# A streaming add-and-GELU kernel: wider chunks, longer store rows, and a first store that is issued later

## The chip, the cores and the metric

One core of one Trainium2 chip. The metric is the device time of one launch in microseconds. All runs quoted here were fast, with a granted clock of 1.0. The span is the part of a launch that is profiled, from the program's first instruction to its last. Differences in this case are of the order of 0.5%, so every comparison has four to six timed runs of the changed kernel and six to eleven of the kernel before, in alternation and, on each occasion, on one chip. A ratio is the mean time of one kernel's fast runs over that of the other's of the same rounds, so it is not quite the ratio of the medians quoted beside it; it comes with its 95% interval.

## The reference

```python
# x, y: (1024, 4096) float32
z = x + y
out = 0.5 * z * (1 + np.tanh(np.sqrt(2 / np.pi) * (z + 0.044715 * z ** 3)))
```

33.55 MB are read and 16.78 MB written. The kernel uses 0.5 (1 + tanh(u)) = sigmoid(2u), so an element takes an add, a square, a scalar-tensor operation, a sigmoid and a multiplication.

## The kernel before

Each of the 128 partitions holds eight rows, 32,768 columns, in one SBUF tile `z`. All transfers are issued by one sequencer (SP) on one queue. The adds run on GpSimd (the first on VectorE), squares and sigmoids on ScalarE, the other two operations on VectorE; `w` is in PSUM.

```python
    YS = 8192
    CH = 1024
    PS = 4
    loads = [2048, 6144, 8192, 8192, 8192]
    stores = [8192, 8192, 8192, 4096, 4096]
    # ... pools: z for all columns, two y buffers of YS columns, PS PSUM buffers of CH columns
    def store(i):
        a, b = sr[i]
        nc.sync.dma_start(out=ov[:, a:b], in_=zt[:, a:b])
    # ...
    sp = []
    for i in range(len(loads)):
        sp += [(load_x, i), (load_y, i)]
    sp += [(store, i) for i in range(len(stores))]
    # ...
    for i in range(-3, C + 1):
        if 0 <= i < C:
            dve.append((stt, i))
            acts.append((sig, i))
        if 0 <= i - 1 < C:
            dve.append((mul, i - 1))
        # ...
        if 0 <= i + 2 < C:
            acts.append((sq, i + 2))
    # ...
        store: lambda i: [(mul, c) for c in over(cr, *sr[i])],
```

## Time and profile before

| | before |
|---|---|
| device time, median | 122.09 us |
| span of the profiled run | 119.9 us |
| share of the 16 DMA engines' span filled by the one queue | 98.4% |
| first store issued / last load complete | 60.5 us / 80.7 us |
| last compute instruction ends | 103.9 us |

Three more lines of the page and the timeline of the kernel before matter later. The first counts packets, the second is a second DMA queue (its packets, MB, share of the engines' span), the third the issue of the stores (start, length, instruction, number).

```profile
DMA packets 2162, 50.35 MB, mean 420 GB/s; under 512 B 240, under 2 KB 240, under 8 KB 240
...
q14 instruction: 2, 0.02, 0.0%
```

```profile
60.52 43.78 SPq L131 DMA_DIRECT2D out_dram<-z  x5
```

Of 2162 packets, 2160 carry data or completions. The other two are 8 KB each on the queue that brings instructions.

### The profile page before, as it was taken

The numbers are of one execution on the slowest core, as the hardware profiler recorded it, in microseconds if no ns is written. First come the engines' busy times: TensorE is split into PE (matmuls) and PEld (weight loads), VectorE is DVE, ScalarE is ACT, GpSimd is POOL, SyncE is SP. The second block draws the span as 40 slices with busy tenths as digits, with TensorE's granted clock in tenths as the row PEclk, the third lists the DMA queues.
The fourth block names the chain that finished last, engine by engine and source line by source line (L and its number), as shares of the span: only waits on it lengthen the run. The fifth ranks groups of instructions, "written<-read, shape, count | busy, mean of one in ns | idle before, by whom it ended". The sixth has DMA issues, their size and how long they took to land.

```text
span 119.9 us, 247 instructions
## 1 busy us (share of the span) xinstructions
DVE 75.5 (63%) x66; ACT 63.8 (53%) x66; POOL 73.0 (61%) x35
## 2 busy tenths in 40 slices
DVE  0044700049999109999996999996899999600000
ACT  4006300078876038788867887884888887200000
POOL 0046000699990199999969999959999991000000
DMA  6999999989898999999898989999998989998995
GB/s 191 424 478 410 476 426 394 514 361 514 361 503 372 481 394 448 426 426 448 383 492 372 503 350 514 361 383 481 388 481 372 492 383 481 394 470 366 437 426 224
DMA packets 2162, 50.35 MB, mean 420 GB/s; under 512 B 240, under 2 KB 240, under 8 KB 240
## 3 DMA queue, kind: packets, MB, share of 16 engines
q1 hardware_dynamic: 2160, 50.33, 98.4%
q14 instruction: 2, 0.02, 0.0%
HBM read 33.55 MB, written 16.78 MB: 420 GB/s over the span
## 4 chain that ended last, share of the span: by engine, by line
DMA 49%; POOL 17%; DVE 16%; SPq 1%; ACT 1%; issue 0%; POOLq 0%
DMA y<-in_y_dram 49%; POOL z L137 17%; DVE z L157 8%; DVE w L148 8%; ACT w L142 1%; SPq L120 1%; SPq L127 1%; POOLq L137 0%
## 5 line engine op out<-in xcount | busy, mean ns | idle before, releaser
L137 POOL TENSOR_TENSOR z<-z,y 128x1024 f32<-128x1024 f32 x31 | 72.8, 2388 | 26.1 <-DMA y<-in_y_dram 26.1
L142 ACT ACTIVATE w<-z 128x1024 f32<-128x1024 f32 x32 | 32.9, 1028 | 37.3 <-POOL z L137 31.3
L148 DVE SCALAR_TENSOR_TENSOR w<-w,z 128x1024 f32<-128x1024 f32 x32 | 39.4, 1233 | 21.0 <-ACT w L142 21.0
L157 DVE TENSOR_TENSOR z<-w,z 128x1024 f32<-128x1024 f32 x32 | 38.8, 1215 | 0.0
L153 ACT ACTIVATE w<-w 128x1024 f32<-128x1024 f32 x32 | 31.4, 981 | 0.4 <-DVE w L148 0.4
L137 DVE TENSOR_TENSOR z<-z,y 128x1024 f32<-128x1024 f32 x1 | 1.2, 1226 | 6.1 <-DMA y<-in_y_dram 6.1
L196 ACT ACT_TABLE_LOAD x1 | 1.3, 1283 | 1.3 <-PEq L228 1.3
L195 DVE MEMSET one<- 128x1 f32 x1 | 0.1, 59 | 1.3 <-PEq L228 1.3
L228 POOL MEMSET const-float32-0.0<- 128x1 f32 x1 | 0.1, 98 | 0.2 <-issue 0.2
L196 ACT ACTIVATE one<-one 128x1 f32<-128x1 f32 x1 | 0.2, 203 | 0.0
L228 POOL MEMSET const-bfloat16-1.0<- 128x1 bf16 x1 | 0.1, 101 | 0.0
L228 POOL MEMSET const-uint8-127<- 128x1 uint8 x1 | 0.1, 101 | 0.0
L228 POOL MEMSET const-float32-1.0<- 128x1 f32 x1 | 0.1, 98 | 0.0
## 6 DMA issues: line engine op xcount, KB each, us to landing
z<-in_x_dram SPq DMA_DIRECT2D x3, 4096.0 KB, 34.2
y<-in_y_dram SPq DMA_DIRECT2D x3, 4096.0 KB, 24.8
out_dram<-z SPq DMA_DIRECT2D x3, 4096.0 KB, 30.2
out_dram<-z SPq DMA_DIRECT2D x2, 2048.0 KB, 17.3
z<-in_x_dram SPq DMA_DIRECT2D x1, 3072.0 KB, 13.4
y<-in_y_dram SPq DMA_DIRECT2D x1, 3072.0 KB, 20.4
z<-in_x_dram SPq DMA_DIRECT2D x1, 1024.0 KB, 4.9
y<-in_y_dram SPq DMA_DIRECT2D x1, 1024.0 KB, 7.0
```

What stands on the lines that cost most here:

```text
L120: nc.sync.dma_start(out=zt[:, a:b], in_=xv[:, a:b])
L127: nc.sync.dma_start(out=yt[s][:, o : o + b - a], in_=yv[:, a:b])
L137: eng.tensor_add(out=zt[:, a:b], in0=zt[:, a:b], in1=yt[s][:, o : o + b - a])
L142: nc.scalar.activation(out=wt[c], in_=zt[:, a:b], func=act.Square, scale=root)
L148: nc.vector.scalar_tensor_tensor(out=wt[c], in0=wt[c], scalar=c1, in1=zt[:, a:b], op0=alu.add, op1=alu.mult)
L153: nc.scalar.activation(out=wt[c], in_=wt[c], func=act.Sigmoid)
L157: nc.vector.tensor_mul(out=zt[:, a:b], in0=wt[c], in1=zt[:, a:b])
L195: nc.vector.memset(one, 0.0)
L196: nc.scalar.activation(out=one, in_=one, func=act.Sigmoid)
L228: nc = _bacc.Bacc("TRN2", target_bir_lowering=False, num_devices=1)
```

## The change

Its intent: fewer, longer instructions and rows, and stores that join the queue only when the loads are nearly through. Cut to its core:

```diff
-    CH = 1024
-    PS = 4
+    CH = 2048
+    PS = 2
     loads = [2048, 6144, 8192, 8192, 8192]
-    stores = [8192, 8192, 8192, 4096, 4096]
+    FIRST = 8
+    stores = [16384, 8192, 4096, 4096]
 ...
-        nc.sync.dma_start(out=ov[:, a:b], in_=zt[:, a:b])
+        ins = nc.sync.dma_start(out=ov[:, a:b], in_=zt[:, a:b])
+        if i == 0:
+            tc.add_manual_dep(ins.ins, muls[FIRST].name, ...)
 ...
-    for i in range(-3, C + 1):
-        ...
+    acts = [(sq, 0), (sq, 1)]
+    for c in range(0, C, 2):
+        dve += [(stt, c), (stt, c + 1), (mul, c), (mul, c + 1)]
+        acts += [(sig, c), (sig, c + 1)]
+        if c + 2 < C:
+            acts += [(sq, c + 2), (sq, c + 3)]
 ...
-        store: lambda i: [(mul, c) for c in over(cr, *sr[i])],
+        store: lambda i: [(mul, c) for c in over(cr, *sr[i])] + [(mul, FIRST)],
```

More of the change, by code (lines that the diff above doesn't have):

```diff
@@ L115 @@
     zt = pool_sb.tile([P, TOT], fp32, tag="z", name="z")
-    yt, wt = {}, {}
+    yt, wt, muls = {}, {}, {}
     def load_x(i):
@@ L130, in store @@
         a, b = sr[i]
-        nc.sync.dma_start(out=ov[:, a:b], in_=zt[:, a:b])
+        ins = nc.sync.dma_start(out=ov[:, a:b], in_=zt[:, a:b])
+        if i == 0:
+            tc.add_manual_dep(
+                ins.ins,
+                muls[FIRST].name,
+                mybir.DependencyInfo(mybir.DependencyClass.Sync, mybir.DependencyReason.DATA),
+                reason="the stores join the queue when the last load is nearly done",
+            )
     def add(c):
@@ L156, in mul @@
         a, b = cr[c]
-        nc.vector.tensor_mul(out=zt[:, a:b], in0=wt[c], in1=zt[:, a:b])
+        muls[c] = nc.vector.tensor_mul(out=zt[:, a:b], in0=wt[c], in1=zt[:, a:b]).ins
     sp = []
@@ L164 @@
     pool = [(add, c) for c in range(C) if c in by_pool]
-    dve, acts = [], []
-    for i in range(-3, C + 1):
-        if 0 <= i < C:
-            dve.append((stt, i))
-            acts.append((sig, i))
-        if 0 <= i - 1 < C:
-            dve.append((mul, i - 1))
-        if 0 <= i + 3 < C and i + 3 not in by_pool:
-            dve.append((add, i + 3))
-        if 0 <= i + 2 < C:
-            acts.append((sq, i + 2))
+    dve = [(add, c) for c in range(C) if c not in by_pool]
+    acts = [(sq, 0), (sq, 1)]
[4 more added lines that the diff above has]
+            acts += [(sq, c + 2), (sq, c + 3)]
     needs = {
```

## The prediction

> **What bounds the kernel now.** I read the page first, the slices (part 2) before the groups of instructions, because no compute engine there is busy over two thirds of the span.
>
> ```profile
> DVE 75.5 (63%) x66; ACT 63.8 (53%) x66; POOL 73.0 (61%) x35
> ...
> DVE  0044700049999109999996999996899999600000
> ACT  4006300078876038788867887884888887200000
> POOL 0046000699990199999969999959999991000000
> DMA  6999999989898999999898989999998989998995
> ...
> q1 hardware_dynamic: 2160, 50.33, 98.4%
> ...
> HBM read 33.55 MB, written 16.78 MB: 420 GB/s over the span
> ```
>
> Every compute engine has holes; the DMA row has none. From the second slice to the last but one it reads 8 or 9, and the one queue's packets fill 98.4% of 16 engines' span. The transfers are the bound, and the bytes (x and y in, the result out) are fixed.
>
> The chain of waits has to be read with this in mind: it follows the last instructions, and its last piece, the final multiplications, ends at 101.64 + 2.30 = 103.9 us of a span of 119.9. The last 16 us are stores alone. The waits of the DMA queue's own sequencer and the chain tell whether the queue ever runs short of work:
>
> ```profile
> SPq L131 <- DVE z L157: 41.8, 4, 19.4
> SPq L127 <- POOL z L137: 32.6, 2, 18.6
> ```
>
> ```profile
> 2.87 38.57 DMA y<-in_y_dram
> ...
> 41.56 18.51 POOL z L137 x8
> ...
> 60.09 20.58 DMA y<-in_y_dram
> ...
> 101.64 2.30 DVE z L157 x2
> ```
>
> The sequencer waits long, but for transfers that are wanted later. The fourth y load is issued at 60.09 us, when GpSimd has freed its buffer, and in the timeline the first store at 60.52. Both stand behind an x load issued at 36.4, so the engines work on: by stretches, the five from 7 to 104 us move 427, 432, 430, 424 and 433 GB/s. Loads end at about 80.7 us, and stores take the rest. Their last issue is at 104.0, some 16 us before the end, so compute is not what they wait for.
>
> Where do 119.9 us go on a DMA engine? The trace's packet records give the median of one row: 309 ns for 8 KB, 611 for 16, 912 for 24, 1213 for 32. That is a line: (1213 - 309) / 3 = 301.3 ns per 8 KB, and about 8 ns a packet. One engine (an equal sixteenth of the packets) has 16 x 0.309 + 16 x 0.912 + 72 x 1.213 + 16 x 0.611 us, and 15 completion packets of 9 ns: 116.8 us. Beside this there is 1.5 us before the first packet, 0.6 us per engine by which the first load packets are longer than the median, and **0.46 us per engine at 77 to 80 us, where the last two load packets of many engines are longer (up to 1.87 us) as the engines turn from loads to stores**. The completions of the last load come over 0.76 us instead of 0.54, those of the later stores over 0.9. So some 0.5 to 1 us is all that scheduling of the stores could ever recover.
>
> **What the Trainium skill says.** "DMA: Bandwidth & Descriptors", section "Where 436 GB/s comes from", has 435.2 GB/s as the ceiling of the 16 ports; the trace agrees (32 KB in 1.213 us on 16 engines is 432 GB/s), so a full engine has no faster rate to find. The same page, "Queues, rings and completion order", says that an engine consumes descriptors in ring order; the trace agrees, stores of 4 MB being 30.2 us from issue to landing in the median, where 4 MB alone take about 10. "GPSIMD Engine Reference", section 3.1, has 4497 ns on GpSimd and 2293 ns on the vector engine for an add of 2048 fp32 columns. Those are my durations for the new shapes; the trace has 2388 and 1226 ns for 1024, so the doubled ones fit. "SBUF — State Buffer", section "Who interferes with whom", says that a vector instruction with two SBUF inputs contends with a GpSimd one that reads SBUF: at 7.5 us the trace has both adding, and GpSimd's first took 3.39 us instead of about 2.3.
>
> **The change, part by part.**
>
> *Chunks of 2048.* Each engine has half the instructions at about twice the length. Starts of consecutive vector instructions lie 1.14 to 1.15 us apart in the timeline, and the second 1024 columns cost 2293 - 1226 = 1067 ns more by the two figures above; so one of 2048 takes 1.145 + 1.067 = about 2.2 us, against 2.29 for two. ScalarE goes from 0.96 to an estimated 1.9 (at most twice), GpSimd from 2.31 to about 4.5. With 64 vector instructions turned into 32, this saves 32 x 0.08 = 2.6 us of vector time, and GpSimd 15 x 0.1 = 1.5; none of it is on the path, since transfers set the end. The first add becomes 2048 on the vector engine with no GpSimd add beside it: also hidden.
>
> *Two PSUM buffers, pairs.* The order list has squares for c and c+1, two scalar-tensor operations, two sigmoids, two multiplications. The square of c+2 now waits for the multiplication of c. With 2.2 us of the other multiplication to cover a square of 1.9, the vector engine should stay nearly full, 8.8 us per pair against 9.0 of GpSimd adds. This coarsens the pipeline, and chunk 15 finishes later: from the last y at 80.7, four adds of 4.5 end at 98.9; square 100.8, scalar-tensor 103.1, two multiplications 107.5. That is 3.5 us later than before, but the stores behind it need it only at about 115.
>
> *The late store.* It waits for chunk 8's multiplication, the third of its group of four vector instructions. The x and y for it land at 61.0 (GpSimd's start in the trace). Adds of chunks 8 and 9 end at 65.6 and 70.1; the square of 9 at 72; its scalar-tensor at 74.3; the multiplication of 8 follows at 76.5. So the store is issued at about 76.6 rather than 60.5. From first issue to first packet the trace took 1.5 us: data at about 78. The engines finish their loads at 80.0 to 80.7, so they should find the store there, **with about 2 us to spare**. The next stores: chunk 11 is done at about 88 (the first store occupies the queue until 100), chunk 13 at 98.5 (needed at 110), chunk 15 at 107.5 (needed at 115). No hole.
>
> *64 KB rows.* 128 / 16 = 8 rows per engine replace 16 of 32 KB: by the line, 2419 ns instead of 2 x 1213, saving 8 x 0.008 = 0.06 us, and one completion packet less. Together **0.07 us**.
>
> Sum: -0.07 us, and between -0.5 and +0.5 for how the turn from loads to stores goes. I take -0.1: 122.0.
>
> **The rivals.** (1) *The turn gets cheaper.* If the longer packets at 77 to 80 us and the uneven completions come from the store descriptors lying behind the loads for 17 us, the late issue removes them: 0.5 us, 121.5 at best perhaps 121.2. For it: the excess lies exactly at the turn. Against: descriptors also lie queued from 36 us on without any excess, and the store is to be there before the turn in both kernels. (2) *The queue runs dry.* If the pair order costs more than I counted, or if a store with such long rows takes longer to start, each us beyond 80 us is a us lost on all engines: 2 us late would give 124. For it: a margin of only 2 us, hanging on six dependent instructions. Against: all six have measured durations. (3) *64 KB rows are slower or get split.* A split in two gives the old time; anything odd at this size would show in 8 rows per engine, 10% over their 19.4 us being 2 us. The line from 8 to 32 KB gives no sign of it. (4) *Compute becomes the bound at the end.* It would need chunk 15 to come 7 us later than worked out; unlikely.
>
> **Range and chances.** The spread of three runs is 0.02 us, other boots perhaps 0.3%. Rivals 1 and 2 set the ends: 121.3 to 122.8. Faster by 2% means 119.6 us or less, below what 116.8 us of packets and the fixed ends allow: 0.01. Slower by 2% needs a hole of 2.4 us by rival 2 or 3: 0.04.
>
> **What would show it.** DMA row without a hole, queue share still above 98%; first store issued at 76 to 78 us; completions of the last load at the same time as before, near 80.7; packets of 64 KB at about 2.42 us; last vector instruction at 107 to 108; GpSimd adds near 4.5 us. A gap between the last load packet and the first store packet proves rival 2; the excess at 77 to 80 us gone proves rival 1.

## The result

The changed kernel takes **121.61 us** (median of 6, 121.37 to 121.98) against 122.09 (6 runs): ratio 0.9965, interval 0.9942 to 0.9988. That is 0.4 us faster: well under 2%, and inside the range. The page of the changed kernel:

```profile
DVE 73.7 (62%) x34; ACT 61.0 (51%) x34; POOL 67.5 (56%) x19
...
DMA  6999999989898999989898989998899889999996
...
DMA packets 2016, 50.33 MB, mean 420 GB/s; under 512 B 224, under 2 KB 224, under 8 KB 224
...
q1 hardware_dynamic: 2016, 50.33, 98.6%
...
L145 POOL TENSOR_TENSOR z<-z,y 128x2048 f32<-128x2048 f32 x15 | 67.3, 4519 | 31.1 <-DMA y<-in_y_dram 31.1
L156 DVE SCALAR_TENSOR_TENSOR w<-w,z 128x2048 f32<-128x2048 f32 x16 | 36.7, 2296 | 26.4 <-ACT w L150 26.1
```

The DMA row has no hole in either kernel, and the queue's share hardly moved. All 2016 packets are the data queue's: **there is no q14 line here any more**. From its timeline, the issue of the stores and the last multiplications:

```profile
76.44 31.41 SPq L132 DMA_DIRECT2D out_dram<-z  x4
...
103.01 4.48 DVE L165 TENSOR_TENSOR z<-w,z 128x2048 f32<-128x2048 f32 x2
```

The first store goes out 16 us later than before, and compute ends at 107.5 us instead of 103.9. Neither made the kernel slower.

The profiled executions do not show where the 0.4 us went: that of the kernel before, from another occasion than the six runs, happened to be a quick one (121.73 us, below their median), that of the changed kernel a slow one (121.92, above its own). A gain as small as the scatter of one kernel's runs can't be read off one pair of profiles. It needs runs that take the parts apart.

### The profile page after: what moved, and what is told of

Read it like the earlier page. It is cut to its first block, busy times and chain, and to the rows that moved or that the text cites. A ratio compares the mean times of both kernels' runs of the same rounds, so it can differ in the third digit from the quotient of the medians.

```text
span 119.8 us, 174 instructions
## 1 busy us (share of the span) xinstructions
DVE 73.7 (62%) x34; ACT 61.0 (51%) x34; POOL 67.5 (56%) x19
## 2 busy tenths in 40 slices
DMA packets 2016, 50.33 MB, mean 420 GB/s; under 512 B 224, under 2 KB 224, under 8 KB 224
## 3 DMA queue, kind: packets, MB, share of 16 engines
q1 hardware_dynamic: 2016, 50.33, 98.6%
## 4 chain that ended last, share of the span: by engine, by line
DMA 50%; POOL 26%; POOLq 4%; DVE 4%; DVEq 2%; ACT 2%; SPq 1%; issue 0%
DMA y<-in_y_dram 50%; POOL z L145 26%; POOLq L215 4%; DVE w L156 2%; DVEq L215 2%; DVE z L165 2%; ACT w L150 2%; SPq L121 1%; SPq L128 1%; POOLq L145 0%
## 5 line engine op out<-in xcount | busy, mean ns | idle before, releaser
L145 POOL TENSOR_TENSOR z<-z,y 128x2048 f32<-128x2048 f32 x15 | 67.3, 4519 | 31.1 <-DMA y<-in_y_dram 31.1
L156 DVE SCALAR_TENSOR_TENSOR w<-w,z 128x2048 f32<-128x2048 f32 x16 | 36.7, 2296 | 26.4 <-ACT w L150 26.1
L150 ACT ACTIVATE w<-z 128x2048 f32<-128x2048 f32 x16 | 30.1, 1882 | 38.3 <-POOL z L145 29.3
L165 DVE TENSOR_TENSOR z<-w,z 128x2048 f32<-128x2048 f32 x16 | 35.8, 2281 | 0.0
L161 ACT ACTIVATE w<-w 128x2048 f32<-128x2048 f32 x16 | 29.7, 1855 | 4.4 <-DVE w L156 4.4
L145 DVE TENSOR_TENSOR z<-z,y 128x2048 f32<-128x2048 f32 x1 | 2.3, 2293 | 6.1 <-DMA y<-in_y_dram 6.1
```

Of the source, the lines that this page charges most:

```text
L145: eng.tensor_add(out=zt[:, a:b], in0=zt[:, a:b], in1=yt[s][:, o : o + b - a])
L150: nc.scalar.activation(out=wt[c], in_=zt[:, a:b], func=act.Square, scale=root)
L156: nc.vector.scalar_tensor_tensor(out=wt[c], in0=wt[c], scalar=c1, in1=zt[:, a:b], op0=alu.add, op1=alu.mult)
L161: nc.scalar.activation(out=wt[c], in_=wt[c], func=act.Sigmoid)
L165: muls[c] = nc.vector.tensor_mul(out=zt[:, a:b], in0=wt[c], in1=zt[:, a:b]).ins
```

## The experiments

Two numbers from the packet records are used in all of them. The **excess at the turn** is the sum of what the 32 KB packets that are over 0.02 us too long add to the normal 1.213 us, starting in the 4.4 us before the last load's last completion packet, divided by 16 engines. The **spread at the end** is the time between the first and the last engine's completion of the last store; the launch ends with the last (in the kernel before, its signal arrives at 119.7 us of a span of 119.9).

Starting theories: **A**, only the packets count (0.07 us). **B**, the long rows bring the gain. **C**, the late issue brings it. **D**, the fewer instructions bring it.

### One part at a time

Rows alone, on the kernel before:

```diff
-    stores = [8192, 8192, 8192, 4096, 4096]
+    stores = [16384, 8192, 4096, 4096]
```

> The kernel before with one store of 64 KB rows for the first half, issued as soon as its chunks are done (about 64 us), chunks of 1024 as before. Theory A (packets only): 8 rows per engine of 2.418 us replace 16 of 1.213, and one completion packet goes: 0.07 us faster, so ratio 0.9994, not told from 1. Theory B (the row length is what made the change 0.4 us faster): ratio about 0.9965.

Measured 122.15 us, ratio 1.0007 (0.9994 to 1.0021). The interval leaves the 0.07 us of theory A just possible, and excludes B.

The late issue alone, on the kernel before, with its own chunks and rows:

```diff
+    FIRST = 19
+        if i == 0:
+            tc.add_manual_dep(ins.ins, muls[FIRST].name, ...)
-        store: lambda i: [(mul, c) for c in over(cr, *sr[i])],
+        store: lambda i: [(mul, c) for c in over(cr, *sr[i])] + [(mul, FIRST)],
```

> The kernel before with only the late issue: its five stores of 32 KB and 16 KB rows, the first held until chunk 19 of 1024 is multiplied (76.0 us in the trace of before, against 60.5). Theory A: nothing, ratio 1.000, the longer packets at 77 to 80 us stay at 0.4 to 0.6 us per engine. Theory C (the late issue made the change faster): ratio about 0.9965, and fewer or shorter long packets at the turn.

Measured 122.09 us, ratio 1.0004 (0.9989 to 1.0019). The store was issued at 75.7 us. The excess at the turn was 0.99 us, more than before, not less. C fails at this hour of issue.

Chunks alone (`CH = 2048`, `PS = 2`, the paired order; stores as before, not held):

> Chunks of 2048 in pairs with two PSUM buffers, the stores as before and issued when ready. Theory A: ratio 1.000, last vector instruction at about 107.5 us as in the changed kernel. Theory D (fewer instructions, hence fewer accesses beside the transfers, made it faster): ratio about 0.9965.

Measured 122.05 us, ratio 0.9997 (0.9982 to 1.0012). The device time is unchanged, though this kernel has no instruction packets. D alone fails too. (Its span did fall; see "All runs together".)

Chunks and rows together, not held (the changed kernel without its wait):

```diff
-        if i == 0:
+        if False:
-        store: lambda i: [(mul, c) for c in over(cr, *sr[i])] + [(mul, FIRST)],
+        store: lambda i: [(mul, c) for c in over(cr, *sr[i])],
```

> The changed kernel without its late issue: chunks of 2048, 64 KB rows for the first half, issued when its own chunks are done (chunk 7, about 68 us). Theory A: 0.9994 as for the rows alone. Theory C: 1.000, the gain is gone with the gate. Theories B and D: 0.9965, as with the gate.

Measured 122.11 us, ratio 1.0005 (0.9988 to 1.0021). No single part, in these forms, nor these two together, gives the gain. Either the first comparison was scatter, or the wait pays only in company.

### The whole again, and the wait moved

> The changed kernel unaltered, a second time. Neither the rows, nor the late issue, nor the chunks alone, nor chunks and rows together, came out faster. Theory A (packets only): 0.07 us faster, ratio about 0.9994, and the 0.9965 of the first comparison was its scatter of runs. Theory E (the late issue pays only together with the long rows): ratio 0.9965 again, 121.6 us.

Measured 121.57 us against 121.92, ratio 0.9965 (0.9948 to 0.9982): the same ratio on another occasion. Theory A is out; the gain is real.

Next the wait was moved by one chunk (`FIRST = 9`):

> The changed kernel with its first store held until chunk 9 is multiplied instead of chunk 8, so issued at 78.6 instead of 76.4 us. The first packet of the run came about 1.5 us after the first issue. If the store needs 1.5 us to start, its data are there at 80.1, just as the first engines end their loads (80.0): theory A says 0 to 0.5 us slower than with chunk 8. If theory E holds because the best moment is the last one, it is as fast or faster.

Measured 121.42 us, **ratio 0.9945** (0.9927 to 0.9963): the fastest of all, and faster than what it was expected to be. No packet at the turn is too long (excess 0.00), and all 16 engines end within 0.31 us of each other, where the kernel before has 0.90.

And by one more (`FIRST = 10`), which must starve the queue:

> The changed kernel with its first store held until chunk 10 is multiplied, so issued at about 85.4 us. The queue must run dry: data at 86.9 by a start of 1.5 us, where the loads end at 80.0 to 80.7, so 6 to 7 us slower, about 128 us, with a hole in the DMA row. This measures the margin that the prediction gave as 2 us.

Measured 127.98 us, ratio 1.0488 (1.0470 to 1.0507). Two-microsecond stretches of this run: stretch and length, then busy time of VectorE, ScalarE and GpSimd, clock, DMA share and GB/s.

```profile
78.00:80.00 2.00, 2.00 (x2) 1.42 (x2) 0.84 (x1) 1.00 0.61 262
80.00:82.00 2.00, 1.94 (x2) 2.00 (x2) 1.69 (x1) 1.00 0.00 0
82.00:84.00 2.00, 2.00 (x2) 1.50 (x2) 2.00 (x1) 1.00 0.00 0
84.00:86.00 2.00, 2.00 (x2) 1.62 (x2) 2.00 (x2) 1.00 0.00 0
86.00:88.00 2.00, 2.00 (x2) 1.24 (x1) 2.00 (x1) 1.00 1.23 524
```

The last two columns are the point: six microseconds without a byte. The page's DMA row shows the same hole as two zeros:

```profile
DMA  6999999989999798997989989007977797797997
```

The run gives two constants. The store was issued at 85.31 us and its first packet came at 86.15: a start of **0.84 us**. And with no store in the queue at all, the engines' completion packets of the last load lie at **79.3 to 79.7 us**, against 79.6 to 80.4 in the kernel before. So the long packets at the turn do cost time, and the 78.5 us of `FIRST = 9` puts the store's first packet at 79.4, just as the first engines come free.

The next expectation has 86.58, 1.27 and 79.7 to 80.1 for these. Its packet times lie about 0.4 us later than the trace has them beside the timeline's issues. Packets compared with packets are not touched by that; a start, which runs from an issue to a packet, is.

### The late issue without the rest

With that, the late issue alone was tried again on the kernel before, one chunk of 1024 later (`FIRST = 20`, otherwise the edit of the run with 19):

> The kernel before with its own chunks of 1024 and its own stores of 32 and 16 KB rows; only the first store is held, until chunk 20 is multiplied: issued at 78.0 us, one chunk (2.3 us) later than in the earlier run with the late issue alone, which showed nothing at 75.7. Idle-queue start was 1.27 us (85.31 to 86.58), so its data come at 79.3, against undisturbed loads ending 79.7 to 80.1. Theory L (what counts is that the store arrives in less than about one packet, 1.2 us, before the loads end; rows and chunks don't matter): no long packets at the turn (under 0.15 us per engine), ratio 0.995, 121.4 us. Theory E (the late issue pays only with the long rows): ratio 1.000 and long packets as before.

Measured 121.68 us, ratio 0.9978 (0.9963 to 0.9992); the store was issued at 78.3 us. The excess at the turn is 0.00, as theory L says, so neither rows nor chunks are needed for that. But only 0.2% came of it, not 0.5%. Its engines complete the last load within 0.50 us of each other. After the first store 14 of them still lie within 0.47 us; the other two are at 0.72 and 1.18, and the last stays behind to the end. Something held those two during that store. The page says what else was on the engines:

```profile
q1 hardware_dynamic: 2160, 50.33, 98.2%
q14 instruction: 2, 0.02, 0.0%
```

In the packet records the two instruction packets start at 84.4 and 87.0 us, 0.309 us each, and beside them lie data packets of 1.519, 1.326 and 1.685 us in place of 1.213. Every run with chunks of 1024 has two such packets, starting between 83.7 and 89.3 us; of those with chunks of 2048 so far, none. That makes theory **Q**: the longer instruction streams need one more fetch, the DMA engines serve it between data packets, and the launch ends with the engine that is last.

### Instructions put back

Test of Q: the kernel with `FIRST = 9`, and idle instructions of one column that bring VectorE and ScalarE back to the length they have in the kernel before (66 instructions each on the page; the expectation says 68 rows).

```diff
     def sig(c):
         nc.scalar.activation(out=wt[c], in_=wt[c], func=act.Sigmoid)
+        for _ in range(2):
+            nc.scalar.activation(out=one, in_=one, func=act.Sigmoid)
 ...
+        for _ in range(2):
+            nc.vector.memset(pad, 0.0)      # behind each multiplication
```

> The changed kernel with the first store held until chunk 9 (the fastest so far, 121.42 us), plus two memsets of one column behind each multiplication and two activations of one column behind each sigmoid, which bring VectorE and ScalarE back to the 68 rows of instructions that the kernel before has. All kernels with chunks of 1024 show two 8 KB packets of the instruction queue at 84 to 90 us, none with chunks of 2048 does. Theory Q (these cost the engine that moves them about 0.6 to 0.8 us, and the end is that of the last engine): the two packets come back, the last completions spread over about 1 us instead of 0.31, and the time is 121.7 to 121.9 us. If the instruction queue has no part in it: 121.4 to 121.5.

> The changed kernel with the first store held until chunk 9, unaltered, a second time, beside the run with the instructions added: 121.4 us, ratio 0.995, no instruction packets after the start, under 0.1 us per engine of excess at the turn.

Measured 121.91 us (ratio 0.9992, 0.9978 to 1.0005) with the idle instructions, and 121.45 us (0.9954, 0.9942 to 0.9967) without. The page of the first:

```profile
q1 hardware_dynamic: 2016, 50.33, 98.1%
q14 instruction: 2, 0.02, 0.0%
```

and of the second:

```profile
q1 hardware_dynamic: 2016, 50.33, 98.7%
```

The two packets are back (82.5 and 94.6 us), the spread at the end is 0.88 us in place of 0.37, and 0.46 us are lost. The store of the first was issued at 78.9 us and no packet at the turn is too long. The idle instructions themselves lie on engines that end well before the last store. Q holds. The idle instructions also delay the store by 0.3 us, but little of the loss is that: after the first store 14 engines complete within 0.18 us, the other two 0.69 and 1.01 us after the first, and at the end the last of those 14 is 0.08 us later than the last engine of the other profile, the last of all 0.79 us.

**Is the last engine one that served a fetch?** Two sets of completion packets answer it, those of the last load and those of the store behind it, during which the instruction packets come. In the kernel before, 14 of the 16 engines take 9.68 us from the one to the other. Only two take longer, and one of these two is the last of all, at 90.20 us, where the last of the other 14 is at 90.06. So it is in every profile with instruction packets: the last completion is one of the two that lag. It lies 0.14 to 0.40 us behind the other 14 while the turn is uneven (before, rows alone, chunk 19), and 0.71 and 0.83 us behind where the turn is clean (chunk 20, idle instructions). In the chunks alone, the chunks and rows and the changed kernel, all without instruction packets, the completions of all 16 engines shift alike, within 0.001 us (0.06 in the changed kernel's second profile).

### Does each turn cost?

Two runs put a store among the loads. In the first, the 4 MB store goes ahead of the last y load:

```diff
-    stores = [8192, 8192, 8192, 4096, 4096]
+    stores = [8192, 8192, 8192, 4096, 2048, 2048]
-    sp += [(store, i) for i in range(len(stores))]
+    sp = sp[:-1] + [(store, 0)] + sp[-1:]
+    sp += [(store, i) for i in range(1, len(stores))]
```

> The kernel before with the first 4 MB store put into the queue ahead of the last y load (and the last 4 MB of stores as three, so that compute, 10 us later, does not hold them up). It makes the engines turn from loads to stores twice and back once. If each turn from load to store costs the 0.46 us per engine seen at 77 to 80 us, it is 0.46 us slower, plus whatever a turn back costs, 0.06 for the additional packets: about 122.6 us. If the longer packets are only the way in which the records show the change of direction and no time is lost, it is the same as before, 122.1.

Measured 122.25 us, ratio 1.0016 (0.9999 to 1.0034): less than the 122.6 expected. The excess was 0.67 us at the first turn from loads to stores, but 0.05 at the second, although the second store too had waited in the queue for over 20 us.

In the other, a store of 2048 columns goes between two loads at 27.9 us:

```diff
-    stores = [8192, 8192, 8192, 4096, 4096]
+    stores = [2048, 6144, 8192, 8192, 4096, 4096]
-    sp += [(store, i) for i in range(len(stores))]
+    sp = sp[:7] + [(store, 0)] + sp[7:]
+    sp += [(store, i) for i in range(1, len(stores))]
```

> The kernel before with a small first store (2048 columns) put into the queue between two loads, at about 28 us, so that it moves at about 51 us; the other stores are not held. Theory F (only the first store of the run makes the loads ahead of it longer; the run with a store ahead of the last y load had 0.66 us per engine of excess at its first turn and under 0.1 at its second, though that store too had been queued for 20 us): excess of about 0.5 us at 48 to 52 us, and less than 0.15 at the turn at 80 us; time as before or up to 0.1 slower for the additional packets. Theory I (each turn from queued loads to queued stores costs it): about 0.5 us at both turns, time 0.5 us longer, 122.5.

Measured 122.30 us, ratio 1.0028 (1.0013 to 1.0043). At the small store each engine has one load packet of 1.89 to 2.39 us in place of 1.21 (excess 1.00 us); at the large turn, 32 us later, there is none. Theory F holds for where the cost lies: **it falls on the loads ahead of the first store of the run, once.** The time went a little above the 0.1 us that F allowed. Why the first store does this is not shown. That it does not happen when the loads are nearly through as the store arrives is shown by five profiles (`FIRST = 9` twice and with idle instructions, 10, and 20 with chunks of 1024).

### All runs together

| kernel | first store issued, us | 8 KB instruction packets | excess at turn, us | spread at end, us | span less that of before, us | time outside the span, us | ratio of times |
|---|---|---|---|---|---|---|---|
| before | 60.5 | 2 | 0.44 | 0.90 | 0 | 1.83 to 1.86 | 1 |
| rows alone | 66.9 | 2 | 0.44 | 0.86 | +0.04 | 1.85 | 1.0007 |
| late issue alone, chunk 19 | 75.7 | 2 | 0.99 | 1.10 | +0.02 | 1.83 | 1.0004 |
| chunks alone | 59.7 | 0 | 0.89 | 0.67 | -0.42 | 2.19 | 0.9997 |
| chunks and rows | 67.9 | 0 | 1.28 | 0.56 | -0.32 | 2.17 | 1.0005 |
| changed kernel, two occasions | 76.4 | 0 | 0.53, 0.19 | 0.87, 0.61 | not listed, -0.79 | 2.15, 2.19 | 0.9965, 0.9965 |
| late issue alone, chunk 20 | 78.3 | 2 | 0.00 | 1.07 | -0.27 | 1.83 | 0.9978 |
| `FIRST = 9` with idle instructions | 78.9 | 2 | 0.00 | 0.88 | -0.08 | 1.86 | 0.9992 |
| `FIRST = 9`, two occasions | 78.5, 78.6 | 0 | 0.00, 0.01 | 0.31, 0.37 | -0.99, -0.88 | 2.17, 2.19 | 0.9945, 0.9954 |
| `FIRST = 10` | 85.3 | 0 | 0.00 | 0.15 | +5.61 | 2.18 | 1.0488 |
| store ahead of the last y load | 47.3 | 2 | 0.67 | 1.28 | +0.19 | 1.84 | 1.0016 |
| small store at 28 us | 27.9 | 2 | 1.00 | 0.99 | +0.35 | 1.83 | 1.0028 |

Excess and spread are of the one profiled execution of each kernel; the excess is that of the run's first turn. They explain the order only where they are far apart; the values of the early stores, 0.44 to 1.28, have no order that these runs explain. The spans are means of all runs of the occasion.

The column beside the ratios holds a surprise. Time less span is 1.79 to 1.89 us in every listed run of the kernels with two instruction packets and 2.12 to 2.22 us in every run of those without, whatever else they do; the idle instructions bring back the lower value with the packets. So dropping the fetch takes time out of the span, and **about 0.35 us come back outside it**. The traces hold only the span: what happens in these 0.35 us is not shown.

## Why the prediction was right, and where its reasons were not

- **The bound** was named rightly: no hole in the DMA row, the queue's share 98.4% before and 98.6% after, and of 3.6 us later compute nothing reaches the end.
- **The late store** came as worked out: issue predicted at 76.6 us, measured 76.44; last vector instruction predicted 107.5, measured 107.5; GpSimd adds of 4.5 us, measured 4.52. The margin of 2 us was the right size, in part by luck. The start was put at 1.5 us, where the trace has 1.00 for the first load and 0.84 for a store; the loads' end was put at 80.0, where undisturbed engines are free from 79.3. The two errors cancel: first packet at an estimated 76.44 + 0.84 = 77.3, 2 us before 79.3. One chunk later there is none left, two chunks later cost 6 us.
- **The rows**: 2419 ns predicted for 64 KB, 2418 in the records. Alone they changed nothing that could be measured.
- **The turn** was the term that was mis-sized. The prediction put -0.1 us on rows and turn together (measured: -0.4 for the whole change), with -0.5 to +0.5 for the turn, and its argument against rival 1 was that "the store is to be there before the turn in both kernels". That was true, and it was the wrong test: what counts is whether the store comes more than a packet or two before the loads are through. At 77.3 us it comes so near to the end that part of the excess is gone (0.19 and 0.53 us in two profiles; 0.99 with the store issued 0.7 us earlier). Rival 1 was the right one, in part: 121.6 is where it pointed, though by the prediction's own test (the excess gone) only the later stores show it: `FIRST = 9`, and chunk 20 with chunks of 1024.
- **The chunks** were said to have "none of it on the path". Their compute time is indeed hidden. But they also shorten the instruction streams, and that takes two packets off the DMA engines when only the last engine counts. The prediction left out the q14 line of the page, which it could have read.
- **The range** held, but one of its supports did not: "the spread of three runs is 0.02 us" became 0.46 us between the lowest and the highest of six. And the y load of 60.09 us is the fifth and last, not the fourth; nothing hangs on that.
- **Why each part alone gave nothing or little.** The rows alone are worth 0.07 us at most, by their interval. The late issue at chunk 19 came too early; at chunk 20 it gives 0.27 us. Dropping the fetch is worth what the fetching engine lies behind the others, less the 0.35 us outside the span: 0.14 to 0.40 us behind with an uneven turn, so about nothing (chunks alone, 0.9997); 0.71 us with a clean turn, so an estimated 0.36 us more than the late issue's 0.27, 0.63 in all. `FIRST = 9` measured 0.65 and 0.55 (differences of means). In the changed kernel itself the wait is what pays: chunks and rows without it are at 1.0005, with it at 0.9965.

The version with `FIRST = 9` beats both kernels, by 0.5% against before on both occasions. Its store comes with no margin: one chunk later it costs 6 us.

## What to carry to other kernels

When the transfers fill 98% of the span, look at what is uneven between the DMA engines: the last completion ends the launch, and of two causes that delay different engines, each can hide what mending the other is worth. Compare spans as well as times: here a gain inside the span came back as a loss outside it. A transfer queued early is not always free; here the first store was cheapest when it came just as the loads ended, at the price of a margin under one chunk. Read the lines that say 0.0% too: a second queue's two packets put one engine 0.1 to 0.8 us behind.

## What the Trainium skill lacked or had wrong

- "Runtime: NRT & Kernel Launch", section "Instruction fetch mechanics", says that an instruction stream is refilled in blocks of 16 KiB and that the cost of crossing a block is mostly hidden. The two packets of 8 KB agree with the block. The cost is not hidden where the DMA engines are the bound: 121.91 us with them, 121.45 without, and the last engine 0.7 us further behind (spread 0.50 us before, 1.18 us after the first store of the late-issue run with chunk 20).
- "DMA: Bandwidth & Descriptors", section "Two DMAs through the same engine are not ordered", says that descriptors start in order but are pipelined, with separate read and write sides. That would let a queued store act on loads that are still under way, and fits the long packets, but no run shows that this is their cause. It has nothing on a cost: 0.19 to 1.28 us per engine at the first store of a run that was queued 2 us or more ahead, 0.05 or less at the next turn.
- No page has it that a store issued as the loads end is better than one queued 18 us ahead: 0.2% here alone (chunk 20), 0.5% together with the wider chunks (`FIRST = 9`).
- No page has it that the time outside the span goes with the instruction streams: 1.79 to 1.89 us with the two packets, 2.12 to 2.22 us without.
